# One decoder layer on one core: weight pieces of one megabyte, modulation vectors in one go, mixer constants in slots, decay columns apart

## The chip, the cores and the metric

The kernel runs on one core of a Trainium2 chip. The metric is the device time of one execution in microseconds: the median of several runs, three of the kernel before.

## What is computed

One layer of a decoder trunk for 256 tokens of width 2048, all in float32. A condition vector c is turned into six modulation vectors; the layer mixes tokens in three parallel branches (a causal pooling, a stick-breaking attention with 8 heads, a linear attention with 4 heads and a decay that depends on the data), gates and adds the branches, and ends with a gated feed-forward of width 5632.

```python
mod = silu_c @ w_ada + b_ada                    # shift, scale, gate, twice
h = _rmsnorm(x, g_norm1) * (1.0 + sc1) + sh1
proj = h @ w_in                                 # u_pool, q/k/v_sb, q/k/v/r_gla, a_low (16 columns), 3 x 2048 gates
log_alpha = log_sigmoid(a_low @ w_a2 + b_a2) / GLA_TAU
merged = sum_i sigmoid(g_i) * (branch_i @ W_br_i)
x = x + ga1 * (merged @ w_out)
h = _rmsnorm(x, g_norm2) * (1.0 + sc2) + sh2
x = x + ga2 * ((silu(h @ w_gate) * (h @ w_up)) @ w_down)
```

## The kernel before

**Products.** Everything is kept transposed: x and h are 16 chunks of 128 channels by 256 tokens. TensorE's float32r operands hold fewer bits than float32, so each operand is split into hi (a rounded copy, made by ScalarE) and lo (what is left, a subtraction on VectorE). `mm3` multiplies hi by hi, hi by lo and lo by hi in three matmuls of 256 columns; `mm2` does the first two in one matmul of 512 columns, since an operand's hi and lo lie side by side.

**Weight pieces.** `load` (L65) takes a buffer of `wraw`, which has six of 1056 columns (528 KB), and SP issues the DMA. `split_w` (L71) makes hi (L77) and lo (L78) of the whole piece, in `whi` and `wlo` with three buffers each; the raw buffer is free after lo. Nearly all pieces have 1024 columns, 512 KB: a block of 128 output columns over 2048 channels is two pieces. `w_per` has pieces of 768 columns, v of the linear attention pieces of 1056.

**Modulation vectors.** w_ada lies transposed, so each of the 96 columns of 128 channels is a product with c, which every partition holds, summed along the row: `ada_half` (L170) loads half a vector (512 KB) and VectorE multiplies and sums it in one instruction (L173); the second half starts from the sum of the first. The 32 vectors of the first norm are made in `modulate` (L211), the others from a queue, `ada_q`, some halves at each call of `ada` (L181): in `proj_v`, after each gate, after each branch block, after blocks of the output projection and after each `gated`.

**Stages, in the order of the program.**
- The first norm.
- For each chunk n: `modulate(n + 1)` in steps between the products of chunk n. `persistent` adds chunk n to six pairs of columns that stay in PSUM; from n = 4 on, `extra` makes 14 other pairs over groups of four chunks, summed in SBUF. At n = 14 the mixers' constants are loaded (L265).
- The last group of the 14 extra pairs (L539), each followed by `steps`, then v with the 16 columns of the decay's rank behind it (L544: 528 columns, as two halves of 264, in four accumulators), then the gates of the first eight blocks.
- The mixers are generators: a piece of work, then a `yield` with a cost. `steps(n)` (L497) runs up to n pieces of those that are due; each goes in two blocks or more after what feeds it. The linear attention's steps (`gla_level`, `gla_diagonal`, `gla_cross`) can't begin before `gla_decay` is through, and that waits for `gl["a"]`, which is set behind v (L553). It loads `w_a2` (L330) and turns the 16 columns round by matmuls with the identity (L333).
- The other gates, branch products and merge (L592); the output projection with the residual (L624 to L640, L632 is the last block's update of x); the second norm (L641), whose chunks `modulate2` makes; the feed-forward, whose first three blocks go chunk by chunk; and w_down (L682).

A scheduler puts the instructions of each engine in an order by its own estimate of when each is ready; instructions that come first in the program have priority. At run time each engine works through its queue in that order. `slots` has 62 buffers of 128x512 for everything else.

## Time and profile before

| | us |
|---|---|
| median of three runs | 1560.77 (1560.53 to 1561.52) |
| span of the profiled execution | 1558.6 |
| TensorE busy in it | 1518.9 (97%) |
| VectorE busy | 1130.8 (73%) |
| ScalarE busy | 739.7 (47%) |

The profile is of one execution, which has its own span, a little under the time of a run. DMA engines move 377 MB, 242 GB/s on average. A busy share is an average over stages with different limits, so the rows further down go by stretches: TensorE's gaps in each, what ended them, and what the other engines and the DMA queue did meanwhile. Times within the span are counted in microseconds from its start.

### The profile page before, as it was taken

Reading aid. Unit: us, or ns where it says so; the run is one execution under the profiler, and the core shown is the slowest. Engines: PE = TensorE matmul, PEld = TensorE weight load, DVE = VectorE, ACT = ScalarE, POOL = GpSimd, SP = SyncE. Lnnn points to the kernel's source line nnn. Section 1 sums busy time; section 2 is a strip of 40 time slices with the busy share of each in tenths; the row PEclk is TensorE's granted clock in tenths of the full one; section 3 lists DMA queues with packets and bytes.
Section 4 is the critical chain, followed back from the end, with each engine's and each line's share of the span. In section 5 each row is a group of like instructions: output and inputs, shape, how many; then the busy total and the mean of one; then the engine's idle time right before and its main releaser. Section 6 shows DMA issues by size and latency. Waiting matters only on the chain.

```text
span 1558.6 us, 26019 instructions
## 1 busy us (share of the span) xinstructions
PE 1518.9 (97%) x10304; PEld 1398.8 (90%) x10304; DVE 1130.8 (73%) x1671; ACT 739.7 (47%) x1028; POOL 1.9 (0%) x11
## 2 busy tenths in 40 slices
PE   5899999989999999999989999999999999999999
PEld 4899998989999999999877888888888888888888
DVE  7889979988877889898878666665555555545443
ACT  4454456465565434444445444444444444333333
POOL 0000000000000000000000000000000000000000
PEclk9899999999999999999999999999999999999999
DMA  9999984855768999997865777776666665666663
GB/s 329 372 328 326 332 276 136 287 193 194 243 215 280 323 342 345 351 314 230 285 208 196 234 239 229 241 230 188 189 189 189 188 189 176 207 192 202 190 207 95
DMA packets 108556, 377.17 MB, mean 242 GB/s; under 512 B 12049, under 2 KB 15249, under 8 KB 108433
## 3 DMA queue, kind: packets, MB, share of 16 engines
q1 hardware_dynamic: 108434, 375.52, 73.5%
q8 instruction: 80, 1.31, 0.3%
q14 instruction: 42, 0.34, 0.1%
HBM read 373.37 MB, written 2.10 MB: 241 GB/s over the span
## 4 chain that ended last, share of the span: by engine, by line
PE 91%; DVE 4%; DMA 2%; ACT 1%; issue 1%; SPq 0%; DVEq 0%; ACTq 0%
PE acc L108 34%; PE acc L109 18%; PE acc L92 9%; PE acc L90 9%; PE acc L91 9%; PE mx L90 3%; PE mx L91 3%; PE mx L92 3%; PE mx L239 3%; DVE raw L173 1%; PE acc L533 1%; DVE lo L78 1%; PE mx L377 1%; DMA raw<-in_w_ada_dram 1%; ACT s L39 1%
## 5 line engine op out<-in xcount | busy, mean ns | idle before, releaser
L78 DVE TENSOR_TENSOR lo<-raw,hi 128x1024 fp32r<-128x1024 f32 (+2 forms) x528 | 627.4, 1190 | 316.9 <-ACT hi L77 315.5
L77 ACT CAST hi<-raw 128x1024 fp32r<-128x1024 f32 (+2 forms) x528 | 539.3, 1023 | 653.6 <-issue 208.4
L108 PE MATMUL acc<-s,hi 128*128 128x512 f32 x2308 | 806.6, 394 | 5.5 <-DVE s L652 4.4
L109 PE MATMUL acc<-s,lo 128*128 128x256 f32 x2308 | 650.1, 282 | 1.2 <-DVE lo L78 1.1
L108 PEld LDWEIGHTS acc<-s,hi 128*128 128x128 f32 x2308 | 434.1, 188 | 104.5 <-issue 4.7
L109 PEld LDWEIGHTS acc<-s,lo 128*128 128x128 f32 x2308 | 434.7, 188 | 2.3 <-DVE lo L78 2.1
L90 PE MATMUL acc<-s,hi 128*128 128x256 f32 x1212 | 346.3, 286 | 14.2 <-ACT hi L77 14.1
L92 PE MATMUL acc<-s,lo 128*128 128x256 f32 x1212 | 344.6, 285 | 0.9 <-DVE lo L78 0.9
L91 PE MATMUL acc<-s,hi 128*128 128x256 f32 x1212 | 343.5, 284 | 0.0
L90 PEld LDWEIGHTS acc<-s,hi 128*128 128x128 f32 x1212 | 232.0, 191 | 16.3 <-ACT hi L77 15.6
L92 PEld LDWEIGHTS acc<-s,lo 128*128 128x128 f32 x1212 | 231.3, 191 | 2.9 <-DVE lo L78 2.2
L91 PEld LDWEIGHTS acc<-s,hi 128*128 128x128 f32 x1212 | 231.5, 191 | 0.2 <-issue 0.2
L173 DVE CUSTOM_DVE_ANT_0 raw<-raw,cs,mod 128x1024 f32<-128x1024 f32 x96 | 122.9, 1280 | 35.9 <-DMA raw<-in_w_ada_dram 35.1
L173 DVE CUSTOM_DVE_ANT_0 raw<-raw,cs,vt 128x1024 f32<-128x1024 f32 x96 | 122.8, 1279 | 29.3 <-DMA raw<-in_w_ada_dram 29.0
L90 PE MATMUL mx<-s,hi 128*128 128x256 f32 x384 | 110.0, 287 | 0.0
L91 PE MATMUL mx<-s,hi 128*128 128x256 f32 x384 | 108.3, 282 | 0.0
L92 PE MATMUL mx<-s,lo 128*128 128x256 f32 x384 | 108.0, 282 | 0.0
L39 ACT ACTIVATE s<-s 128x256 f32<-128x256 f32 (+2 forms) x167 | 83.5, 518 | 48.3 <-DVE s L662 34.7
L90 PEld LDWEIGHTS mx<-s,hi 128*128 128x128 f32 x384 | 73.2, 191 | 0.7 <-issue 0.5
L91 PEld LDWEIGHTS mx<-s,hi 128*128 128x128 f32 x384 | 72.8, 190 | 0.7 <-issue 0.7
L92 PEld LDWEIGHTS mx<-s,lo 128*128 128x128 f32 x384 | 72.7, 190 | 0.0
L239 PE MATMUL mx<-hi,s 128*128 128x256 f32 x256 | 47.4, 282 | 0.7 <-DVE s L302 0.7
(133 smaller groups left out, 780.5 us busy)
## 6 DMA issues: line engine op xcount, KB each, us to landing
raw<-in_w_ada_dram SPq DMA_DIRECT2D x192, 512.0 KB, 4.9
raw<-in_w_ff_dram SPq DMA_DIRECT2D x176, 512.0 KB, 4.2
raw<-in_w_gate_dram SPq DMA_DIRECT2D x96, 512.0 KB, 4.7
raw<-in_w_down_dram SPq DMA_DIRECT2D x80, 512.0 KB, 4.2
raw<-in_w_ext_dram SPq DMA_DIRECT2D x56, 512.0 KB, 5.2
raw<-in_w_br_dram SPq DMA_DIRECT2D x32, 512.0 KB, 5.0
raw<-in_w_out_dram SPq DMA_DIRECT2D x32, 512.0 KB, 4.5
raw<-in_w_per_dram SPq DMA_DIRECT2D x32, 384.0 KB, 5.0
```

The costliest lines, as they stand in the source:

```text
L39: r = nc.scalar.activation(out, in_, func, **kw)
L77: nc.scalar.copy(hi, raw)
L78: vec.tensor_tensor(lo, raw, hi.bitcast(F32), ALU.subtract)
L90: mm(out, lhsT=wh, rhs=x[:, :T], start=first, stop=False, skip_group_check=True)
L91: mm(out, lhsT=wh, rhs=x[:, T:], start=False, stop=False, skip_group_check=True)
L92: mm(out, lhsT=wl, rhs=x[:, :T], start=False, stop=last, skip_group_check=True)
L108: mm(out, lhsT=hi[:, k * P:(k + 1) * P], rhs=x, start=first, stop=False, skip_group_check=True)
L109: mm(out[:, :T], lhsT=lo[:, k * P:(k + 1) * P], rhs=x[:, :T], start=False, stop=last, skip_group_check=True)
L173: vec.tensor_tensor_reduce(raw, raw, cs[:, i * 1024:(i + 1) * 1024], 1.0, init, ALU.mult, ALU.add, mod[:, t, i:i + 1])
L239: mm(m[:, b * T:(b + 1) * T], lhsT=l, rhs=r, start=first and i == 0, stop=last and i == 2, skip_group_check=True)
L377: mm(m[:, i * w:(i + 1) * w], lhsT=k[:, i * P:(i + 1) * P], rhs=q[:, i * w:(i + 1) * w], start=True, stop=True)
L533: mm(m[b][c][:, :w], lhsT=xs, rhs=ws[:, o:o + w], start=f, stop=l)
```

## The change

`wraw` gets four buffers of 2048 columns (1 MB) instead of six of 1056. A weight piece is up to 1 MB, one block of 2048 channels; the class `Weights` loads it at once and splits it in parts of 1024 columns (768 in `w_per`), each when it is first used. A modulation vector is one load and one instruction over 2048 columns (for chunk 0 two of each); `ada` counts halves in `due` and takes a vector when two are due. `modulated` replaces the chunk's modulation in both norms: a product with scale and rstd on VectorE, the shift with rounding on ScalarE, the rest on VectorE. The constants (`ct`, `mneg`, `mk`, and `w_a2`) get slots and are loaded at n = 14. The decay's 16 columns leave v, which has 512 columns now in two accumulators; they get 16 matmuls of their own ahead of the last extra pieces, with 48 stationary columns (hi, zeros, lo) and the 512 columns of h, so they come out turned already. `extra` works on two pairs at a time.

```diff
-WW = 1056
+WW = 2048
+PART = 1024
-    wraw = ctx.enter_context(tc.tile_pool(name="wraw", bufs=6))
+    wraw = ctx.enter_context(tc.tile_pool(name="wraw", bufs=4))
...
-    def split_w(src):
...
+    class Weights:
+        def __init__(self, src, part=PART):
+            self.raw, self.part, self.made = load(src), part, {}
+
+        def at(self, col, n):
+            i = col // self.part
+            if i not in self.made:
+                raw = self.raw[:, i * self.part:min((i + 1) * self.part, self.raw.shape[-1])]
+                hi, lo = (p.tile([P, PART], F32R, tag=t, name=f"{t}{next(names)}")[:, :raw.shape[-1]]
+                          for p, t in ((whi, "hi"), (wlo, "lo")))
+                nc.scalar.copy(hi, raw)
+                vec.tensor_tensor(lo, raw, hi.bitcast(F32), ALU.subtract)
+                self.made[i] = hi, lo
+            col -= i * self.part
+            return tuple(p[:, col:col + n] for p in self.made[i])
...
-    def ada_half(t, i):
-        raw = load(w_ada[t, i])
-        init = vt[:, V_ADA + t:V_ADA + t + 1] if i == 0 else mod[:, t, 0:1]
-        vec.tensor_tensor_reduce(raw, raw, cs[:, i * 1024:(i + 1) * 1024], 1.0, init, ALU.mult, ALU.add,
-                                 mod[:, t, i:i + 1])
+    def ada_vec(t, parts=1):
+        raw = wraw.tile([P, WW], F32, tag="raw", name=f"raw{next(names)}")
+        w = D // parts
+        for i in range(parts):
+            nc.sync.dma_start(raw[:, i * w:(i + 1) * w], w_ada[t, :, i * w:(i + 1) * w])
+        for i in range(parts):
+            p = raw[:, i * w:(i + 1) * w]
+            vec.tensor_tensor_reduce(p, p, cs[:, i * w:(i + 1) * w], 1.0,
+                                     mod_col(t) if i else vt[:, V_ADA + t:V_ADA + t + 1], ALU.mult, ALU.add, mod_col(t))
...
     def ada(n):
+        due[0] += n
+        while due[0] >= 2 and ada_q:
+            due[0] -= 2
+            t = ada_q.popleft()
+            ada_vec(t)
...
+    def modulated(xk, g, r, b):
+        f, t = slot()[:, :T], slot(F32R)
+        vec.scalar_tensor_tensor(f, xk, g, r, ALU.mult, ALU.mult)
+        act(t[:, :T], f, AF.Identity, bias=b)
+        vec.scalar_tensor_tensor(t[:, T:], f, b, t[:, :T].bitcast(F32), ALU.add, ALU.subtract)
+        return t
...
         if n == 14:
-            nc.sync.dma_start(ct, consts)
+            ct, mneg, wa2 = slot()[:, :T], slot()[:, :384], slot()
+            mk = slot().bitcast(U8)[:, :1024].rearrange("p (a t) -> p a t", a=8)
+            tri, up = ct[:, :P], ct[:, P:]
+            nc.sync.dma_start(ct, consts[:, :T])
+            nc.sync.dma_start(mneg, consts[:, T:])
+            nc.sync.dma_start(wa2, w_a2)
...
-        wa2, aa = slot(), slot()
-        nc.sync.dma_start(wa2, w_a2)
-        m = mx()
-        for b in range(2):
-            mm(m[:, b * P:(b + 1) * P], lhsT=gl["a"][:, b * P:(b + 1) * P], rhs=ident, start=True, stop=True)
-        nc.scalar.copy(aa[:, :T], m[:, :T])
-        vec.memset(aa[32:33, :T], 1.0)
-        yield
+        aa = gl["a"]
...
-    for e in range(14):
-        extra(e, 3)
-        ready.add(e)
-        steps(ST2, 2.6)
-    m = proj_v(w_vg, 528)
-    at = slot()
...
-    gl["a"] = at
+    raw = load(w_a1)
+    hi = whi.tile([P, PART], F32R, tag="hi", name=f"hi{next(names)}")[:, :768]
+    nc.scalar.copy(hi, raw)
+    low = hi.rearrange("p (k c) -> p k c", c=48)[:, :, 32:]
+    vec.tensor_tensor(low, raw.rearrange("p (k c) -> p k c", c=48)[:, :, 32:], low.bitcast(F32),
+                      ALU.subtract)
+    m, aa, t = mx(), slot(), slot()
+    nc.gpsimd.memset(aa[:, :T], 0.0)
+    nc.gpsimd.memset(aa[64:65, :T], 1.0)
+    for k in range(NK):
+        mm(m[:48, :], lhsT=hi[:, k * 48:(k + 1) * 48], rhs=h[k], start=k == 0, stop=k == NK - 1)
+    nc.scalar.copy(t[:48, :T], m[:48, T:])
+    vec.tensor_tensor(aa[:48, :T], t[:48, :T], m[:48, :T], ALU.add)
+    gl["a"] = aa
+    for pair in range(7):
+        for e in extra(pair, 3):
+            ready.add(e)
+            steps(ST2, 2.6)
+    m = proj_v(w_vg, 512)
...
-    ada(len(ada_q) - 32 - 13 * ADA[3])
+    ada(2 * len(ada_q) - due[0] - 32 - 13 * ADA[3])
...
     for half in range(2):
-        w = [split_w(w_ff[j, i, half]) for j, i in firsts]
+        w = [Weights(w_ff[j, i, :, half * 1024:(half + 1) * 1024]) for j, i in firsts]
+        for p in w:
+            p.at(0, P)
```

## Rows read from the trace of the kernel before

**Rows 1.** The page's busy table: us, share of the span, instructions.
```profile
PE 1518.9 (97%) x10304; PEld 1398.8 (90%) x10304; DVE 1130.8 (73%) x1671; ACT 739.7 (47%) x1028; POOL 1.9 (0%) x11
```

**Rows 2.** Stretches: us, busy time by engine (PE first), PEclk, DMA share, GB/s.
```profile
28.00:56.00 28.00, 20.84 (x133) 19.10 (x132) 27.27 (x48) 9.87 (x16) 0.00 (x0) 0.86 0.99 374
56.00:60.00 4.00, 4.00 (x25) 4.00 (x25) 3.58 (x6) 2.12 (x3) 0.00 (x0) 0.67 1.03 412
80.00:235.00 155.00, 155.00 (x1308) 155.00 (x1307) 136.84 (x193) 75.07 (x96) 0.00 (x0) 1.00 0.91 316
235.00:283.00 48.00, 46.21 (x328) 41.31 (x326) 45.04 (x73) 32.50 (x51) 0.00 (x0) 1.00 0.52 164
283.00:317.00 34.00, 31.16 (x224) 28.37 (x223) 32.36 (x70) 16.71 (x26) 0.00 (x0) 1.00 0.75 250
317.00:480.00 163.00, 161.14 (x1328) 157.93 (x1328) 132.31 (x234) 97.20 (x159) 1.05 (x2) 1.00 0.69 221
480.00:700.00 220.00, 219.34 (x1837) 218.36 (x1836) 193.36 (x292) 95.56 (x122) 0.00 (x0) 1.00 0.93 330
804.00:834.00 30.00, 21.38 (x106) 16.81 (x104) 24.77 (x61) 15.92 (x25) 0.00 (x0) 0.89 0.37 125
```

**Rows 3.** Waits of TensorE over the span: us in total, times, longest.
```profile
PE acc L90 <- ACT hi L77: 14.1, 5, 7.2
PE acc L108 <- DVE s L652: 4.4, 1, 4.4
...
PE mx L340 <- DMA s<-in_w_a_dram: 1.7, 1, 1.7
PE mx L298 <- DVE s L481: 1.2, 1, 1.2
```

**Rows 4.** Timeline of VectorE around 42 us: start, us, instruction.
```profile
41.45 1.28 DVE L173 CUSTOM_DVE_ANT_0 raw<-raw,cs,mod 128x1024 f32<-128x1024 f32 x1
...
42.66 1.28 DVE L173 CUSTOM_DVE_ANT_0 raw<-raw,cs,vt 128x1024 f32<-128x1024 f32 x1
```

**Rows 5.** Groups by line, VectorE: busy us, mean ns, idle before.
```profile
L402 DVE TENSOR_TENSOR s<-s 128x512 f32<-128x512 f32 x14 | 9.6, 683 | 0.0
L387 DVE COPY_PREDICATED s<-mk,mx 128x64 f32<-128x64 uint8 x56 | 9.3, 247 | 4.4 <-PE mx L377 4.4
...
L134 DVE SCALAR_TENSOR_TENSOR s<-mx,s 128x512 f32<-128x512 f32 (+1 forms) x12 | 7.5, 641 | 5.1 <-ACT s L39 5.1
...
L406 DVE TENSOR_TENSOR s<-s,s 128x256 f32<-128x256 f32 x14 | 5.9, 421 | 1.6 <-ACT s L39 1.6
...
L294 DVE SCALAR_TENSOR_TENSOR s<-s,vt,s 128x256 f32<-128x256 f32 x8 | 3.8, 475 | 0.0
```

**Rows 6.** DMA issues by line: count, size, median us from issue to landing.
```profile
raw<-in_w_down_dram SPq DMA_DIRECT2D x80, 512.0 KB, 4.2
...
raw<-in_w_down_dram SPq DMA_DIRECT2D x16, 256.0 KB, 3.3
```

**Rows 7.** Pieces of the chain that ended last: start, us, what.
```profile
283.19 11.68 PE acc L533 x96
...
323.94 0.45 PE mx L333 x4
...
816.60 0.23 PE acc L108
```

**Rows 8.** Timeline around the second norm, TensorE and VectorE.
```profile
804.45 0.60 PE L642 MATMUL mx<-s,full 128*128 128x256 f32 x2
805.89 1.28 DVE L173 CUSTOM_DVE_ANT_0 raw<-raw,cs,mod 128x1024 f32<-128x1024 f32 x1 [1.87 <-DMA raw<-in_w_ada_dram]
...
807.10 0.48 DVE L632 SCALAR_TENSOR_TENSOR x<-acc,mod,x 128x256 f32<-128x256 f32 x1
...
822.87 1.28 DVE L173 CUSTOM_DVE_ANT_0 raw<-raw,cs,vt 128x1024 f32<-128x1024 f32 x1
...
825.34 0.40 PE L109 MATMUL acc<-s,lo 128*128 128x256 f32 x1 [0.39 <-DVE lo L78]
```

More of the change, by code (lines that the diff above doesn't have):

```diff
@@ L32 @@
 def kernel(ctx: ExitStack, tc: tile.TileContext, xT, c, vecs, consts, invc, masks, w_ada, w_per, w_ext,
-                      w_gate, w_vg, w_a2, w_pool, w_br, w_out, w_ff, w_down, outT):
+                      w_gate, w_vg, w_a1, w_a2, w_pool, w_br, w_out, w_ff, w_down, outT):
     nc = tc.nc
@@ L228, in extra @@
[L228 to L247 removed]
+        h.append(modulated(x[k], scl[:, k:k + 1], rstd, mod_col(k)))
@@ new lines, in persistent, with extra @@
+    def persistent(k):
+        w = Weights(w_per[k], 768)
+        for t in range(12):
+            mm3(per[t // 2][:, t % 2 * T:(t % 2 + 1) * T], w, t, h[k], k == 0 and t % 2 == 0, k == NK - 1)
+    def extra(pair, g):
+        w = Weights(w_ext[pair, g])
+        for e in (2 * pair, 2 * pair + 1):
+            m = mx()
+            for kk in range(4):
+                xk = h[4 * g + kk]
+                col = e % 2 * 1024 + kk * T
+                for b in range(2):
+                    first, last = kk == 0 and b == 0, kk == 3
+                    if 6 <= e < 10:
+                        xh, xl = xk[:, b * P:(b + 1) * P], xk[:, T + b * P:T + (b + 1) * P]
+                        wh, wl = w.at(col, T)
+                        for i, (l, r) in enumerate(((xh, wh), (xh, wl), (xl, wh))):
+                            mm(m[:, b * T:(b + 1) * T], lhsT=l, rhs=r, start=first and i == 0, stop=last and i == 2,
+                               skip_group_check=True)
+                    else:
+                        mm3(m[:, b * T:(b + 1) * T], w, col // P + b, xk, first, last)
+            if g == 0:
+                ext[e] = slot()
+                nc.scalar.copy(ext[e], m)
+            else:
+                vec.tensor_tensor(ext[e], ext[e], m, ALU.add)
+            yield e
@@ L255 @@
     for n in range(NK):
-        todo = [(persistent, n, 0), (persistent, n, 1)]
+        todo = [(persistent, n)]
         if n >= 4:
-            todo += [(extra, e, n // 4 - 1) for e in range(14 * (n % 4) // 4, 14 * (n % 4 + 1) // 4)]
+            todo += [(lambda p, g: run(extra(p, g)), p, n // 4 - 1) for p in range(7 * (n % 4) // 4, 7 * (n % 4 + 1) // 4)]
         nxt = modulate(n + 1) if n + 1 < NK else iter(())
@@ L594 @@
         sig = sigs[j]
-        hl = [split_w(w_br[j, i]) for i in range(2)]
+        w = Weights(w_br[j])
         brs = [acc(), acc()]
@@ L745, in _layouts @@
     ]
[L748 removed]
+_NAMES = ["xT", "c", "vecs", "consts", "invc", "masks", "w_ada", "w_per", "w_ext", "w_gate", "w_vg", "w_a1", "w_a2", "w_pool",
           "w_br", "w_out", "w_ff", "w_down"]
```

155 lines of the change are left out of this document (53 added, 102 removed).

## The prediction

> **What bounds the kernel now.** I read the busy table first, then the table of stretches, the waits of TensorE, and last the single instructions of the stretches where TensorE isn't full. TensorE is busy 97% of the span [rows 1], so at most 39.7 us of 1558.6 can be won without taking matmuls away. The table of stretches says where they lie [rows 2]: TensorE works 155.00 of 155 us between 80 and 235, and 219.34 of 220 between 480 and 700, and the feed-forward stage has next to no waits either. Weights that arrive in another grain can win nothing there. What is open: the start (20.84 of 28 us, and less before), the stage of the last extra pieces and of v (46.21 of 48 and 31.16 of 34), and the second norm (21.38 of 30). The list of waits agrees [rows 3]: 14.1 us for hi pieces (mostly the start), 4.4 at the second norm, 1.7 for `w_a2`, single waits of about a microsecond on VectorE's mixer steps. So the forecast is a sum of small terms in three places, plus the matmuls that are added.
>
> **The start.** The first chunks need, for each `n`, two modulation vectors (2 MB) and 768 KB of `w_per`. Which is late, the DMA or VectorE? Between 28 and 56 us both are full: VectorE 27.27 of 28 us, DMA share 0.99 at 374 GB/s [rows 2]. VectorE's queue there is a chain without holes: one reduction starts 1.21 us after the one before it [rows 4]. What of it is fixed? A 128x512 subtraction takes 683 ns and a 128x256 multiplication 421 ns [rows 5]: 262 ns for 256 columns, about 1.02 ns a column, and so 1.05 us of the 1.21 for 1024 columns and 0.16 us fixed. Summing a vector in one go saves that 0.16 once per vector, 0.3 us for each `n`. `modulated` gives back a little: two `scalar_tensor_tensor` at 475 ns for a multiplication and a subtraction of about 421 [rows 5], 0.1 us for each `n`. ScalarE loses a cast, but it waits for VectorE here. Net 0.2 us for four chunks (the first vectors stay in two parts), and some of VectorE's 0.7 us of gaps: **-1.0 us**. Bounds: -3.6 (rival 2, below) and +2, if a reduction has to wait for a whole megabyte. For that the rows give a price: 256 KB of `w_down` land in 3.3 us, 512 KB in 4.2 [rows 6], so I estimate 1 MB at 6.0. Four buffers of 1 MB hold more bytes than six of 528 KB, so the DMA queue is fed no worse, and I take the small gain.
>
> **Chunks 4 to 15, gates, feed-forward.** The splits stay 1024 columns wide (768 in `w_per`) and hi and lo keep three buffers, so TensorE's distance from VectorE is unchanged; casts and subtractions are the same in number, save half a column block in v. 0, with TensorE full as cover [rows 2]. If that cover fails it is rival 4. Fewer DMA issues on SP are worth nothing while TensorE is full.
>
> **Matmuls added and removed.** v takes 192 matmuls of 264 columns now; 96 of them last 11.68 us in the chain [rows 7], so all 23.4. After: 96 of 512 columns at 0.23 us, as such a one takes in the chain [rows 7]: 22.1. The decay's rank columns get 16 matmuls of 512 columns of their own, 3.7 us (if 48 stationary columns instead of 128 shortened it in proportion, 1.4; I keep 3.7, the row it is nearest to, since what streams are the 512 moving ones). Away go four transposing matmuls with the identity, 0.45 us [rows 7]. Net **+1.9 us**, all on TensorE.
>
> **The wait for `w_a2`.** Its load moves from `gla_decay` to chunk 14, several extra pieces before its use, so TensorE's 1.7 us at that place [rows 3] go: **-1.7 us**. What is late next there is the mixer step itself, in a stretch where TensorE has 161.14 of 163 us [rows 2]. The other loads at chunk 14 are in SP's queue before, too; `w_a2` adds 256 KB behind `w_per` of the next chunk, under a microsecond of DMA with buffers ahead.
>
> **The order of the mixers' steps.** This is the part with two answers. `gl["a"]` is set before the last extra pieces instead of behind v. Followed by hand through `steps`, the planner then puts the first halves of seven levels and of the crossing (L402, L406, and L407 like L402: 1.8 us of VectorE each [rows 5]), the decay's logarithms, the diagonal and four selections (four copies of L387 each [rows 5]) into the stretch from the first `extra(.., 3)` to the end of v. Together some 19.8 us. Out of it go the norms of heads 5 to 7 (about 2.6 us each: L134, two operations of its kind, two of L294 [rows 5]), and of four pool ends, four outputs and one step of head 5 another 6.3: 14.2. So +5.6 us of VectorE. Four vectors in one go, fewer copies of v and no memset take 1.3 back: +4.3 us, in a stretch where VectorE works 45.04 of 48 and 32.36 of 34 us already [rows 2]. Against that: 4.6 us are free in these 82; the a1 matmuls give VectorE 3.7 us of cover just ahead; and the waits behind v (1.2 us on L481 [rows 3], and one like it on L134) come from the pool and norm work that moves away; also v holds two accumulators instead of four, so a gate can start beside its copies. From +4.3 to -3.2 (all such waits gone). I take **0**, as the two lists balance.
>
> **The second norm.** The chain here [rows 8]: VectorE's reduction at 805.89 waited 1.87 us for a DMA, and the update of x[15] (L632) stood behind it and began at 807.10, though the matmuls behind that block's last one start at 804.45. So about 2.4 us of the path are a vector half that nobody needs yet (a gate of the feed-forward, asked for by the first `gated`) which got in front. After the change `due` counts: 94 halves are asked for by the end of the branches, 47 vectors; the next comes at j = 14, and the one after that only with the second `gated`, behind six half pieces and a whole one, with four buffers. It can't have landed by L632. The one at j = 14 is queued between w_out[14] and w_out[15], some ten microseconds ahead. **-2.4 us**; if a vector still gets in front, it costs 1.8 us more landing and 1.1 more reduction than now, +2.9. After that TensorE's first matmul waits 4.4 us [rows 3] for the norm's chain, whose length stays (multiply, activation, subtraction in both). VectorE has an operation less per chunk, which is worth nothing: TensorE waits for the first chunk alone (one wait in that row). At the half's end the reduction at 822.87 stands in front of lo and costs TensorE 0.4 us [rows 8]; gone: **-0.4**.
>
> **Sum.** -1.0 + 1.9 - 1.7 + 0 - 2.4 - 0.4 = -3.6 us on the span of 1558.6, so 1555.0. The median of the runs is 1560.8, 2.2 us over the span, which I keep: **1557.1 us**. A measurement of this kernel tells about 0.2% from no change, 3.1 us, so the forecast sits near that edge.
>
> **Rivals.**
> 1. *VectorE is the new bound of the mixers' stage.* For it: the 95% above, and the slots. Counting live slots in program order, `ct`, `mneg`, `wa2`, `mk` and the steps that start early raise the peak from 55 to 62, of 62 there are; at the peak an operation, or a pool's load on SP with weights queued behind it, waits for another's end. It decides once VectorE's 4.6 free us can't take 4.3 more. Price 4.3 us, up to 8 with slots: 1561 to 1565, slower. Against: in the gates' stretch VectorE has 132.31 of 163 us. In this rival's stretch the Trainium skill would look for the same sign: its page Perfetto Trace Analysis (section Identifying Performance Opportunities) says that a gap that repeats on the engine that should be full can mean that no buffer is free for the next tile. No run here shows it for slots yet.
> 2. *The pieces are faster, and the start with them.* In 56 to 60 us the DMA moved 412 GB/s [rows 2]; with that instead of 374 over 28 us the start is 2.6 us shorter: 1554.5. Against it: VectorE's 27.27 of 28. The Trainium skill (DMA: Bandwidth & Descriptors, section Bandwidth) has a rule for this: batch to at least 1 MiB for 75% of the peak, which by its table would put 512 KB clearly lower. The trace doesn't agree: many 512 KB pieces in flight hold a share of 0.99, so the grain isn't what holds them back.
> 3. *The late vector doesn't go, another takes its place* (what the change does to the queue is decided by the scheduler's order, not by the text): the -2.4 becomes 0 to +2.9, 1559.5 to 1562.4.
> 4. *Coarse pieces starve TensorE* where VectorE and DMA are both near full (80 to 235, 480 to 700: share 0.91 and 0.93 [rows 2]): a reduction that waits 1.8 us longer, with lo pieces behind it. Lo is two pieces ahead, which covers one such wait and not several: +5 to +8, 1562 to 1565.
>
> **How the numbers follow.** Forecast 0.45 (its own range 1554 to 1560: 0.27 faster, 0.18 the same); rival 1 0.22 (0.07 the same, 0.15 slower); rival 2 0.13 (faster); rival 3 0.12 (0.09 the same, 0.03 slower); rival 4 0.08 (slower). Faster 0.40, the same 0.34, slower 0.26. The range goes from 1552, where rival 2 meets the mixers' good end, to 1565.
>
> **What would show it.** Start: VectorE's reductions about 2.3 us apart and TensorE full a microsecond earlier. v: 96 matmuls of 512 columns, then 16 with 48 stationary ones. No wait on `w_a2`. L632's place: no reduction in front of it. In the mixers' stage: VectorE above 95% and TensorE's waits on lo or mixer steps above 5 us would be rival 1. Waits on hi or lo between 80 and 235 or 480 and 700 would be rival 4. I'm wrong in the step and not the size if the second norm's wait stays, or if TensorE isn't full in a stretch that is full now.

## The result, and the profile after

The changed kernel takes 1573.57 us (median of four runs, 1571.07 to 1586.23), the kernel before in the same comparison 1561.14 us: a ratio of 1.0102, interval 1.0079 to 1.0125. It is slower by 12.4 us; forecast was 1557.1 with a range up to 1565. The profiled execution has a span of 1571.0 us, 12.4 more than before. One thing has to be known to read the numbers below: executions of one and the same kernel of this family can lie in two groups 12 to 14 us apart (three of these four runs are in the lower one, 1586.23 is in the upper), which in the profiles differ in the feed-forward, so that a median or a ratio can be of either group or of a mixture. So I locate gains and losses by stages, each from one profiled execution.

The busy table after the change:

```profile
PE 1525.0 (97%) x10220; PEld 1400.9 (89%) x10220; DVE 1117.2 (71%) x1464; ACT 728.6 (46%) x1010; POOL 2.5 (0%) x13
```

TensorE has 84 matmuls fewer than before [rows 1], and is busy 6 us longer. The table of stretches after (us, busy time by engine from TensorE on, granted clock, DMA share, GB/s), in windows of [rows 2]:

```profile
28.00:56.00 28.00, 18.62 (x132) 17.36 (x131) 25.44 (x34) 8.01 (x12) 0.00 (x0) 0.93 0.97 353
...
80.00:235.00 155.00, 154.29 (x1286) 154.12 (x1285) 132.15 (x156) 68.95 (x84) 0.53 (x1) 1.00 0.86 313
...
283.00:317.00 34.00, 32.83 (x203) 28.69 (x202) 32.08 (x63) 20.82 (x33) 0.00 (x0) 1.00 0.58 202
```

Read two things. Between 28 and 56 us VectorE, which had 27.27 us of work in 28, now has 25.44: it idles, and TensorE with it (for what, is shown further down). And between 80 and 235 us TensorE is busy for 154.29 of 155 us, 0.7 less than before, but has done 22 matmuls fewer, which at 0.12 us each is 2.6 us: the same busy time holds fewer matmuls. TensorE's waits over the span (us in total, times, longest), to be laid beside [rows 3]:

```profile
PE acc L101 <- DVE lo L85: 12.1, 8, 3.0
PE acc L99 <- ACT hi L84: 9.3, 3, 6.7
...
PE acc L553 <- DVE lo L85: 3.3, 2, 2.7
...
PE acc L99 <- ACT s L40: 1.6, 1, 1.6
PE acc L100 <- DVE s L209: 1.2, 1, 1.2
PE acc L553 <- ACT hi L84: 1.1, 1, 1.1
PE mx L670 <- ACT s L40: 0.9, 1, 0.9
```

The wait on `w_a2` is gone. The hi waits of the start fell from 14.1 to 9.3, but 12.1 us on lo (L85) stand there new; v (L553) waits 4.4 us, which before it didn't; L670 is the second norm's last matmul (L643 before) and waits 0.9, where L643 waited 3.0.

**Three landmarks** serve for every comparison below. A: the first VectorE copy of a persistent accumulator (L274 before, L300 after), which ends the first stage. B: the start of the second norm's last matmul. C: the last update of `x`. All in us.

| kernel | A | A to B | B to C | C |
|---|---|---|---|---|
| before | 213.1 | 595.0 | 747.3 | 1555.4 |
| after | 223.7 | 601.1 | 743.1 | 1567.9 |
| difference | +10.6 | +6.1 | -4.2 | +12.5 |

So the loss is in the first stage and in the mixers' and branches' stages. The feed-forward gave some back in this execution, which is of the lower group; kernels whose profile is of the upper group have 755 to 758 for B to C.

### The profile page after: what moved, and what is told of

Read it like the earlier page. It is cut to its first block, busy times and chain, and to the rows that moved or that the text cites. A ratio compares the mean times of both kernels' runs of the same rounds, so it can differ in the third digit from the quotient of the medians.

```text
span 1571.0 us, 24822 instructions
## 1 busy us (share of the span) xinstructions
PE 1525.0 (97%) x10220; PEld 1400.9 (89%) x10220; DVE 1117.2 (71%) x1464; ACT 728.6 (46%) x1010; POOL 2.5 (0%) x13
## 4 chain that ended last, share of the span: by engine, by line
PE 90%; DVE 6%; DMA 2%; ACT 1%; issue 1%; DVEq 0%; ACTq 0%
PE acc L118 34%; PE acc L119 17%; PE acc L101 9%; PE acc L100 8%; PE acc L99 8%; PE mx L99 2%; PE mx L100 2%; PE mx L101 2%; PE mx L259 2%; DVE raw L187 2%; DVE lo L85 1%; DMA raw<-in_w_ada_dram 1%; PE mx L396 1%; ACT s L40 1%; PE acc L553 1%
## 5 line engine op out<-in xcount | busy, mean ns | idle before, releaser
L85 DVE TENSOR_TENSOR lo<-raw,hi 128x1024 fp32r<-128x1024 f32 (+1 forms) x528 | 627.9, 1192 | 376.3 <-ACT hi L84 375.5
L84 ACT CAST hi<-raw 128x1024 fp32r<-128x1024 f32 (+1 forms) x528 | 539.6, 1024 | 664.5 <-PE acc L118 225.6
L99 PE MATMUL acc<-s,hi 128*128 128x256 f32 x1212 | 347.0, 287 | 10.8 <-ACT hi L84 9.3
L101 PE MATMUL acc<-s,lo 128*128 128x256 f32 x1212 | 345.6, 287 | 12.1 <-DVE lo L85 12.1
L99 PEld LDWEIGHTS acc<-s,hi 128*128 128x128 f32 x1212 | 235.0, 194 | 12.8 <-ACT hi L84 10.4
L187 DVE CUSTOM_DVE_ANT_0 raw<-raw,cs,vt 128x2048 f32<-128x2048 f32 (+1 forms) x96 | 223.1, 2325 | 14.4 <-DMA raw<-in_w_ada_dram 14.4
L40 ACT ACTIVATE s<-s 128x512 f32<-128x512 f32 (+2 forms) x165 | 82.6, 521 | 71.4 <-DVE s L684 53.4
L99 PE MATMUL mx<-s,hi 128*128 128x256 f32 x384 | 109.7, 286 | 0.8 <-DVE s L267 0.7
L99 PEld LDWEIGHTS mx<-s,hi 128*128 128x128 f32 x384 | 73.7, 192 | 1.8 <-issue 1.1
L259 PEld LDWEIGHTS mx<-hi,s 128*128 128x128 f32 x256 | 40.3, 192 | 0.2 <-DVE s L144 0.2
```

The costliest lines, as they stand in the source:

```text
L40: r = nc.scalar.activation(out, in_, func, **kw)
L84: nc.scalar.copy(hi, raw)
L85: vec.tensor_tensor(lo, raw, hi.bitcast(F32), ALU.subtract)
L99: mm(out, lhsT=wh, rhs=x[:, :T], start=first, stop=False, skip_group_check=True)
L101: mm(out, lhsT=wl, rhs=x[:, :T], start=False, stop=last, skip_group_check=True)
L187: vec.tensor_tensor_reduce(p, p, cs[:, i * w:(i + 1) * w], 1.0, mod_col(t) if i else vt[:, V_ADA + t:V_ADA + t + 1], ALU.mult, ALU.add, mo ...
```

## The experiments

Theories. S: the start is late because of the grain, the buffers or the order of the work. P: TensorE's spacing is changed by where its operands lie in SBUF, which the change moves (hi and lo shrink from 1056 to 1024 columns, constants leave their tiles, the raw buffers change). M: the early decay makes VectorE the bound at v (rival 1). Rival 4: coarse pieces starve TensorE behind the start.

**Grain undone (e1_grain).**

```
-    wraw ... bufs=4   # tiles of 2048 columns
+    wraw ... bufs=8   # tiles of 1024 columns
-            self.raw, self.part, self.made = load(src), part, {}
+            self.raw = [load(src[:, i:min(i + part, n)]) for i in range(0, n, part)]
-    def ada_vec(t, parts=1):
+    def ada_vec(t, parts=2):   # each half in a buffer of its own
```

> The changed kernel with its raw buffers in the old grain: eight buffers of 1024 columns instead of four of 2048 (the same bytes), every piece loaded in parts of 1024 columns, every modulation vector in two loads and two reductions. Everything else of the change stays (decay apart, constants in slots, modulated, extras in pairs, 62 slots). Theory A, the grain of the pieces makes the loss: the copies of the six pairs in PSUM, which begin at 223.7 us in the changed kernel and at 213.1 before, come back to 212 to 215, the last branch block's first product (732.6 after, 714.9 before) to 717 to 721, and the run to 1558 to 1564 us. Theory B, the order of the extras makes it (chunk 4 has one pair, so TensorE runs dry before chunk 5 is modulated): the copies stay at 220 or later and the run at 1569 or more. Theory C, the decay's earlier place and the slots make it: the copies come back, but the loss between them and the branch stage (some 3 us) stays and grows nothing here; 1562 to 1566.

1583.63 us, ratio 1.0146 (1.0112 to 1.0180). A 218.3, A to B 609.8, B to C 754.9. The old grain gives 5.4 us back at the start (2.4 against the earliest profile of the changed start, 220.7 in e4_late) and then costs 8.7 us behind it. Rival 4 said the reverse of the second.

**Vectors in halves alone (e2_halves).**

```
-    def ada_vec(t, parts=1):
+    def ada_vec(t, parts=2):
```

> The changed kernel with each modulation vector in two loads of 512 KB and two reductions of 1024 columns, in one buffer of 1 MB as before this edit; weights stay in pieces of 1 MB. It takes away the long reduction and the wait for a whole vector, but not the coarse buffers. Theory A1 (VectorE's long reductions block the subtractions and chunk results behind them): most of the 10 us at the start come back, copies at 213 to 217, 1560 to 1565 us. Theory A2 (the buffers' number is what counts, four instead of six, and so the order in which SP can issue): copies stay at 220 to 225, 1569 to 1576 us.

1582.62 us, ratio 1.0135 (1.0094 to 1.0176); three of its four runs are in the upper group. A 220.7, A to B 602.3. As a cause by itself it can't be told from nothing: e4_late, whose first stage is the changed kernel's to the letter, has A at 220.7 too, so a single profile tells nothing under 3 us there.

**Extras 4, 4, 4, 2 (e3_pairs).**

```
-  for p in range(7 * (n % 4) // 4, 7 * (n % 4 + 1) // 4)]
+  for p in range(-(-7 * (n % 4) // 4), -(-7 * (n % 4 + 1) // 4))]
```

> The changed kernel with the seven pairs of extra pieces spread as 2, 2, 2, 1 over each group of four chunks instead of 1, 2, 2, 2; nothing else. Theory B (chunk 4 has too little work while chunk 5 is being modulated): the gap of TensorE between 68.9 and 72.7 us goes, and with it its second slow clock stretch, 4 to 7 us in all; 1566 to 1569. Theory A (the grain): the second pair's megabyte comes in front of chunk 5's vector on the DMA queue, so that chunk comes later by about 2.7 us and what TensorE wins in work it loses in waits: 1570 to 1576.

1578.28 us, ratio 1.0123 (1.0082 to 1.0164). By 80 us it has done 340 matmuls where the changed kernel has 295, but by 210 us it has 1371, as many as that. (Its copies come at 229.3 since one pair more, 48 matmuls, stands ahead of them.) More extras in the first group only move the gap to later chunks.

**The decay handed on behind v (e4_late).**

```
-    gl["a"] = aa          # ahead of the last extras
     m = proj_v(w_vg, 512)
     ...
+    gl["a"] = aa
```

> The changed kernel with the decay's columns handed to the mixers behind v, as before, instead of ahead of the last extra pieces; the 16 matmuls stay where they are. The linear attention's steps then run after v again and fewer slots are live at once. Forecast's rival 1 (VectorE bound in the mixers' stage by the early steps, slots at 62): the stretch from the copies to the first branch product, 298.8 us in the changed kernel and 296.2 before, shrinks by 2 us or more: 1568 to 1571. Theory that the order is worth nothing, as the forecast took it: within 1.5 us of the changed kernel.

1579.88 us, ratio 1.0133 (1.0116 to 1.0151); it sits in the upper group (B to C 756.4). A 220.7, A to B 595.5 against 601.1: 5.6 us, and two more kernels with the early decay and narrow tiles have 602.3 (e2_halves) and 600.3 (e9_between). So handing the decay on early costs that, and v's waits on lo and hi are gone from its list; whether VectorE's work makes the price, as M says, or the slots, this run doesn't separate.

**Hi and lo wide again (e5_wide).**

```
-  hi, lo = (p.tile([P, PART], F32R, tag=t, ...
+  hi, lo = (p.tile([P, 1056], F32R, tag=t, ...
```

> The changed kernel with the tiles of hi and lo 1056 columns wide as before the change (1024 of them used), nothing else: hi at byte 76992 with a pitch of 4224 instead of 4096 bytes, lo and the slots moved by 384 and 768 bytes. Theory A (where the operands lie in SBUF sets TensorE's spacing): 256-column matmuls again 118.7 ns apart on average instead of 120.0 in full stretches, 172 instead of 169 of them in 80 to 100 us, and the total 6 to 7 us shorter, about 1565. Theory B (the spacing comes from something else in the change): 120.0 ns and 169 as in the changed kernel, total 1571 to 1586.

1573.55 us (1573.22 to 1574.43), ratio 1.0079 (1.0059 to 1.0099). The spacing of 256-column matmuls loses its fixed 120 ns (171 of them in 80 to 100 us, 169 in the changed kernel), A to B falls from 601.1 to 596.9, but B to C is 749.9: what the early stages win the feed-forward loses, so the total doesn't move. The place matters; the expected total of 1565 was wrong.

**The kernel before with narrow tiles (e6_narrow).**

```
-WW = 1056
+WW = 1024
-            hi, lo = split_w(src[i])
             for kk in range(2):
+                hi, lo = split_w(src[i][:, kk * n:(kk + 1) * n])
```

> The kernel before with the tiles of raw, hi and lo 1024 columns wide; so that v's pieces fit they come as 16 of 528 columns instead of 8 of 1056. Nothing else is changed. Theory A (place in SBUF sets the spacing): 256-column matmuls 120.0 ns apart, 169 in 80 to 100 us, total about 1565, perhaps with two levels 12 us apart. Theory B: 118.7 ns and 172, total 1558 to 1560 (eight more splits in v cost at most a microsecond).

1565.46 us (1563.13 to 1580.52), ratio 1.0046 (1.0017 to 1.0075). P holds without anything else of the change but narrower raw tiles and v's smaller pieces, though A, at 213.8, moves by 0.7 us only. Two matmuls of the timeline, a hundred apart, in the kernel before (start, us, instruction):

```profile
99.74 0.29 PE L92 MATMUL mx<-s,lo 128*128 128x256 f32 x1
...
111.62 0.28 PE L90 MATMUL mx<-s,hi 128*128 128x256 f32 x1
```

and in e6_narrow:

```profile
99.75 0.28 PE L90 MATMUL mx<-s,hi 128*128 128x256 f32 x1
...
111.75 0.28 PE L91 MATMUL mx<-s,hi 128*128 128x256 f32 x1
```

11.88 against 12.00 us. B to C is 743.9, as in the changed kernel, and the same kernel also ran 1575.27, 1578.74 and 1580.52: the two groups come with the place, too.

**The old start as a whole (e7_start).** On top of e1_grain each half of a vector, each half of the persistent piece and each single extra is back in its place:

```
-        todo = [(persistent, n)]
+        todo = [(persistent, n, 0), (persistent, n, 1)]
-            todo += [... p in pairs, 2, 4, 4, 4 extras to a chunk]
+            todo += [... e one by one, 3, 4, 3, 4 to a chunk]
```

> e1_grain (the changed kernel with loads and reductions of 512 KB in 8 buffers) with the order of the kernel before in the first stage too: each half of a vector, each half of the persistent piece and each single extra piece in its old place in the program, extras 3, 4, 3, 4 to a chunk. Theory C (the start is lost by the order: two reductions in a row ahead of the lo pieces, and a first group of extras that is smaller): the copies of the persistent accumulators, at 213.1 before, 223.7 changed, 218.3 in e1_grain, come at 215 (1.7 of it for the spacing of 120 ns), and the total falls by 3 against e1_grain. Theory D (the shift and the two-operand form of modulated make VectorE's cycle longer): they stay at 218.

1583.80 us, ratio 1.0142 (1.0112 to 1.0172). A 213.4: the start is whole again, even at 120 ns. A to B is 608.4, as in e1_grain. C against D: the order. Two things have to be kept apart here. All these kernels start 1485 matmuls ahead of A; in e7_start TensorE is idle for 20.3 us up to there (before 19.6, e1_grain 22.4) and busy for 193.1 (193.5, 195.9). The idle time is the order's. That the busy time is no longer than before in spite of the 120 ns goes with the clock: granted in 20 to 80 us are 0.97 here and 0.91 in the other two (means of stretches at 1.2 and 2.4 GHz), and one trace doesn't tell whether the order or the execution made that. `modulated`, which is in e7_start, adds no idle time on VectorE in the first four chunks in this order.

**Three good parts in the kernel before (e8_parts).**

```
+    def modulated(xk, g, r, b): ...      # as in the change, in both norms
+            wa2 = slot(); nc.sync.dma_start(wa2, w_a2)     # at chunk 14
-        ada(1)                           # in gated
+        if len(hid) > 2:
+            ada(1)
```

> The kernel before with three parts of the change alone: modulated in both norms, the load of w_a2 at chunk 14, and the reductions of the feed-forward's vectors two gated blocks later (none in front of the update of x[15]). Tiles, pieces and order stay. By the forecast's terms: w_a2 -1.7, second norm -2.4, modulated 0, so 1558.2 - 4.1 = 1554. If modulated lengthens VectorE's cycle in the first chunks (0.58 us a chunk for the wait on ScalarE's shift, five chunks): 1557.

1557.92 us (1554.79 to 1558.80), ratio 0.9980 (0.9967 to 0.9993): faster than both kernels. A 212.4 (-0.7: TensorE's idle time ahead of A grows by 1.2 us, its busy time falls by 1.9 at a granted clock of 0.97 in 20 to 80 us, before 0.91), A to B 593.3 (-1.7), B to C 747.6. Inside A to B the stretch from the last branch product to B fell from 93.2 to 91.1 us, near the 2.4 of the forecast. The wait on `w_a2` is gone as well, and more than given back in the mixers' stage: its list of waits has

```profile
PE acc L92 <- DVE lo L78: 3.1, 7, 1.1
...
PE mx L305 <- DVE s L487: 1.5, 1, 1.5
...
PE mx L485 <- PE mx L299: 1.0, 1, 1.0
```

where before the change lo at L92 cost 0.9 in all, and the waits that answer to L487 and L485 were 1.2 [rows 3] and 0.5. (Of the 3.1 us on lo 1.5 lie in the mixers' stage, the rest in the first.)

**The second vector between the halves, at 1 MB (e9_between).**

```
-    def persistent(k):            # all twelve blocks
+    def persistent(k, i):         # six, and a vector ahead of each call
-        todo = [(persistent, n)]
+        todo = [(persistent, n, 0), (persistent, n, 1)]
```

> The changed kernel, pieces of 1 MB and all, but in the first stage the persistent piece's two halves go in one after the other with a vector in front of each (vector, half, vector, half) as before the change, instead of vector, both halves, vector. Theory C (the order: the second vector's reduction stands behind both lo halves, which wait for ScalarE, which waits for TensorE): the copies of the persistent accumulators come at 215 to 217 instead of 220.7 to 223.7, the total at 1565 to 1568. Theory G (the grain: a reduction that waits for a whole megabyte): they stay at 221 or later.

1582.68 us, ratio 1.0143 (1.0125 to 1.0161), upper group. A 220.1, against 220.7 to 223.7 for the changed start: the order of whole vectors is worth 0.6 to 3.6 us, which a single profile can't tell from nothing.

**Place: e10_pitch, e11_shift, e12_shift128.** All three are e8_parts with the tiles of hi and lo 1152 columns wide; the last two have 256 and 128 unused bytes between lo and the slots.

```
-        hi = whi.tile([P, WW], F32R, ...      # lo likewise
+        hi = whi.tile([P, 1152], F32R, ...
+    nc.gpsimd.memset(pad_p.tile([P, 64], F32, ...), 0.0)     # e11_shift; 32 in e12_shift128
```

> e8_parts with hi and lo tiles 1152 columns wide (4608 bytes, nine times 512) instead of 1056, nothing else: hi, lo and the slots then all start at the same place modulo 512 bytes, as they do in the changed kernel and in e6_narrow, but no longer a power of two apart. If what fixes the spacing is that all operands are a multiple of 512 bytes apart: 120.0 ns without spread, total 1561 to 1564. If it is the pitch of 4096: spread around 118.7 as before, 1557 to 1558.

> e10_pitch with 256 unused bytes in front of the slots, so that weights and moving operands lie half of 512 bytes apart, the same for every buffer. If the relative place of weights and moving operand sets the spacing, it is another fixed value than in e10_pitch, above or below 120.0 ns (117 would be 1551, 122 would be 1568); if only the pitch matters, the same as e10_pitch.

> e10_pitch with 128 unused bytes in front of the slots. As e11_shift: by the theory of the relative place a fixed value of its own, by the theory of the pitch the same as e10_pitch and e11_shift.

e10_pitch: 1572.11 us (1557.53 to 1573.80), ratio 1.0038 (1.0007 to 1.0069); four of its runs are at 1557.5 to 1559.4 and six at 1571.5 to 1573.8. e11_shift: 1571.95 (1571.63 to 1573.74), ratio 1.0074 (1.0057 to 1.0091). e12_shift128: 1563.32 (1561.97 to 1566.80), ratio 1.0023 (1.0013 to 1.0034). Against e8_parts nothing but unused columns and bytes has changed, and the median moves by 5 us and more. With hi, lo and slots equal modulo 512 bytes (e10_pitch) 256-column matmuls are 120.0 ns apart without spread; half of 512 off (e11_shift) they take 117, 118, 120 and 124 ns in equal parts and average 120.0 again; a quarter off, 118.7 early and 119.8 in the gates. So it isn't the pitch of 4096, and the relative place doesn't give each case a value of its own, as the theory had it.

**Halves interleaved at 1 MB (e13_interleaved).** On top of e9_between:

```
-            ada_vec(t, 2 if k == 0 else 1)
-            yield
+            for i in range(2):      # half a buffer each
+                nc.sync.dma_start(p, w_ada[t, :, i * 1024:(i + 1) * 1024])
+                vec.tensor_tensor_reduce(p, p, ...)
+                yield
```

> e9_between with the vectors in halves too (two loads into the halves of a 1 MB buffer, two reductions of 1024 columns), each half's reduction in its old place between the pieces; the weight pieces stay at 768 KB and 1 MB. If the vectors' grain and its order made the start late: the copies of the persistent accumulators at 214 to 216. If it is the weights' grain and four buffers: 219 or later, with waits of TensorE on lo of 2 to 3 us as in the changed kernel.

1595.40 us, ratio 1.0226 (1.0202 to 1.0249). A 236.7, 13 us later than the changed kernel. "219 or later" covers that, but not the reason given for it: TensorE waits 0.3 us on lo there, and 20.1 on hi (L99). What differs from e7_start is that the extras come as pairs and that weights come in 768 KB and 1 MB through four buffers; the next run tries the pairs alone.

**Pairs in the old start (e14_pairs).**

```
-            todo += [... e one by one, 3, 4, 3, 4 to a chunk]
+            todo += [(lambda p, g: run(extra(p, g)), p, n // 4 - 1) for p in ...]
```

> e7_start (512 KB everywhere, old order) with the extras as in the changed kernel, pair by pair, 2, 4, 4, 4 to a chunk instead of 3, 4, 3, 4. If the smaller first group lets TensorE run dry: the copies at 217 or later (213.4 in e7_start). If the vectors' order is what matters: 213 to 215.

1590.28 us, ratio 1.0192 (1.0148 to 1.0235). A 225.5: 12.1 us for the extras alone. TensorE's idle time ahead of A grows by 7.1 of them (27.4 us against 20.3); the other 5.0 are busy time for the same 1485 matmuls, in a trace in which the granted clock falls again after the gaps (0.93 in 80 to 130 us, where e7_start has 1.00). Three windows show where. e7_start:

```profile
0.00:60.00 60.00, 39.74 (x207) 30.97 (x208) 50.96 (x87) 23.14 (x35) 1.49 (x11) 0.97 0.96 358
60.00:80.00 20.00, 20.00 (x169) 20.00 (x168) 16.94 (x25) 9.93 (x14) 0.00 (x0) 1.00 1.00 382
80.00:210.00 130.00, 130.00 (x1086) 130.00 (x1085) 119.50 (x172) 56.35 (x68) 0.00 (x0) 1.00 0.95 335
```

e14_pairs:

```profile
0.00:60.00 60.00, 39.45 (x205) 30.68 (x206) 50.80 (x86) 22.19 (x34) 1.49 (x11) 0.97 0.95 357
60.00:80.00 20.00, 18.18 (x150) 17.78 (x149) 16.29 (x23) 9.21 (x13) 0.00 (x0) 1.00 0.97 355
80.00:210.00 130.00, 124.97 (x1006) 123.77 (x1005) 113.23 (x165) 54.42 (x67) 0.00 (x0) 0.97 0.91 315
```

The changed kernel:

```profile
0.00:60.00 60.00, 35.19 (x174) 28.06 (x175) 48.14 (x66) 21.21 (x33) 1.49 (x11) 0.93 0.93 344
60.00:80.00 20.00, 17.27 (x123) 16.86 (x122) 13.23 (x14) 7.25 (x9) 0.00 (x0) 0.86 0.83 304
80.00:210.00 130.00, 129.29 (x1078) 129.12 (x1077) 114.95 (x135) 58.01 (x72) 0.00 (x0) 1.00 0.89 324
```

and the kernel before:

```profile
0.00:60.00 60.00, 40.42 (x195) 33.05 (x196) 50.22 (x87) 25.17 (x40) 0.86 (x9) 0.91 0.94 348
60.00:80.00 20.00, 20.00 (x171) 20.00 (x170) 16.18 (x22) 11.36 (x16) 0.00 (x0) 1.00 0.95 342
80.00:210.00 130.00, 130.00 (x1098) 130.00 (x1097) 119.30 (x174) 61.55 (x79) 0.00 (x0) 1.00 0.95 335
```

The changed kernel falls behind it by 21, 48 and 20 matmuls in the three windows. In the first 60 us halves and their old order are worth 31 to 33 matmuls, with singles or pairs. From 60 us on, when extras begin, the pairs take 99 matmuls away in e14_pairs. The mechanism is in e14_pairs' timeline of VectorE (start, us, instruction, idle before and its releaser):

```profile
85.69 1.28 DVE L237 CUSTOM_DVE_ANT_0 raw<-raw,cs,mod 128x1024 f32<-128x1024 f32 x1
...
90.36 1.23 DVE L87 TENSOR_TENSOR lo<-raw,hi 128x1024 fp32r<-128x1024 f32 x1 [3.38 <-ACT hi L86]
92.31 1.23 DVE L87 TENSOR_TENSOR lo<-raw,hi 128x1024 fp32r<-128x1024 f32 x1 [0.73 <-ACT hi L86]
93.46 1.28 DVE L237 CUSTOM_DVE_ANT_0 raw<-raw,cs,vt 128x1024 f32<-128x1024 f32 x1
```

L237 is the reduction of half a vector. The next half, at 93.46, stands in program order behind a pair's two lo pieces, and those wait for hi. The next chunk's `h` can't come before it, so TensorE uses up the pair and waits.

**The three suspects undone (e15_undone).** e7_start with hi and lo 1056 wide and `gl["a"]` behind v (the edits of e5_wide and e4_late).

> e7_start with hi and lo 1056 columns wide and the decay's columns handed on behind v: the three suspects undone, everything else of the change kept (a1's matmuls, v in 512 columns, second norm, sums by due, constants in slots). If these three are the whole loss: spread around 118.7 ns, the first branch product at 508 to 511 us, the second norm 2 us shorter, total 1556 to 1560. If something else in the change costs: above 1563.

1572.06 us, ratio 1.0072 (1.0057 to 1.0087). A 212.0, as before the change; but A to B 603.7 and B to C 751.2. The three aren't the whole loss of this kernel. Of its waits (5.0 of the 6.1 us in the first row lie behind the first stage; L675 is the second norm):

```profile
PE acc L103 <- DVE lo L87: 6.1, 8, 1.4
...
PE mx L675 <- ACT s L40: 3.2, 1, 3.2
```

**Old start, large pieces behind it (e16_hybrid, e17_late_wide).** e17_late_wide is the changed kernel with the edits of e4_late and e5_wide. e16_hybrid adds the old start, its halves two to a 1 MB buffer:

```
+    def half(i, src):
+        if i == 0:
+            held_per[0] = wraw.tile([P, WW], F32, tag="raw", ...)
+        r = held_per[0][:, i * 1024:i * 1024 + n]
+        nc.sync.dma_start(r, src)
```

> The changed kernel with the first stage as before the change (vectors, persistent pieces and single extras in halves of 512 KB, two halves to a 1 MB buffer, extras 3, 4, 3, 4), hi and lo 1056 columns wide and the decay handed on behind v; from the last extras on the 1 MB pieces of the change. If the start, the place in SBUF and the early decay are the three costs, and 1 MB pieces do no harm behind the start: copies of the persistent accumulators at 212 to 214, from there to the second norm's matmul 591 to 595 us (603.7 in e15_undone), total 1554 to 1560. If the 1 MB pieces harm there: over 600 us for that stretch, total above 1563.

> The changed kernel with hi and lo 1056 columns wide and the decay handed on behind v (e4_late and e5_wide together), its start untouched. Copies of the persistent accumulators at 220 to 223 as in these two, then 591 to 595 us to the second norm's matmul, total 1564 to 1569: some 10 us above e16_hybrid, which is the start alone.

e16_hybrid: 1564.92 us (1564.52 to 1566.50), ratio 1.0034 (1.0020 to 1.0048); A 217.1, A to B 593.3, B to C 751.0. e17_late_wide: 1571.22 (1569.27 to 1572.05), ratio 1.0076 (1.0061 to 1.0091); A 222.9, A to B 593.6, B to C 750.6. Both totals miss their expectation, and so does A in e16_hybrid (212 to 214), though A to B is as expected. Behind the start 1 MB pieces do no harm: 593.6 against 603.7 for 512 KB pieces. And the start is 5.8 us better with the old order of halves and single extras (idle ahead of A: 22.8 us against 28.2), 5.1 more (e15_undone, idle 19.4) with eight buffers that come free one by one. In the first 60 us of e16_hybrid

```profile
0.00:60.00 60.00, 38.83 (x188) 30.27 (x189) 48.66 (x83) 21.41 (x33) 1.49 (x11) 0.94 0.89 327
```

the DMA engines are busy 0.89 of the time at 327 GB/s, where e7_start has 0.96 and 358. With four buffers that are released as a whole, loads are asked for later: the DMA queue's longest wait for a buffer in 20 to 80 us is 5.0 us, in e7_start 2.9.

## Why the prediction was wrong, step by step

**The start: the step that failed.** Forecast -1.0 (bounds -3.6 to +2), measured +10.6. I costed VectorE's queue as a sum of operations, and its first term was right: a reduction of 2048 columns is followed by the next instruction after 2.27 us (69.92 to 72.19), 0.15 less than two starts 1.21 apart [rows 4]. What it left out is the order in that queue and the place of the extras, for which I wrote no term: the diff turns 3, 4, 3, 4 single extras into 2, 4, 4, 4 in pairs, and halves with other operations between them into whole vectors. VectorE's waits in 20 to 80 us after the change:

```profile
DVE lo L85 <- ACT hi L84: 6.4, 3, 3.4
DVE s L209 <- ACT s L40: 2.9, 5, 0.6
DVE raw L187 <- DMA raw<-in_w_ada_dram: 0.3, 1, 0.3
```

Two of these rows name the step. The second is the shift of `modulated`: "ScalarE loses a cast, but it waits for VectorE here" was half of it, for VectorE then waits for ScalarE, 0.58 us in each of the first five chunks, since nothing stands between the vector's reduction and the rest of `modulated`; four of the five make 2.3 of the 2.6 us that VectorE idles between 28 and 56 us. With vectors in halves the row all but goes (0.3 us in e1_grain). The first row was 3.5 us before the change. The changed kernel's VectorE at 65 us:

```profile
67.78 1.83 DVE L85 TENSOR_TENSOR lo<-raw,hi 128x768 fp32r<-128x768 f32 x2 [2.50 <-ACT hi L84]
69.52 0.48 DVE L207 SCALAR_TENSOR_TENSOR s<-x,scl,s 128x256 f32<-128x256 f32 x1
69.92 2.35 DVE L187 CUSTOM_DVE_ANT_0 raw<-raw,cs,vt 128x2048 f32<-128x2048 f32 x1
```

and its ScalarE:

```profile
66.42 0.59 ACT L265 COPY s<-mx 128x512 f32<-128x512 f32 x1 [5.30 <-PE mx L101]
66.91 1.57 ACT L84 CAST hi<-raw 128x768 fp32r<-128x768 f32 x2
```

The vector that TensorE needs next (69.92) stands behind two lo pieces, these behind their hi, that behind a copy which waits 5.30 us for TensorE's matmuls of the extra. A ring of in-order queues: TensorE feeds the copy, and waits in the end for what is queued behind it (1.57 and 1.16 us, at 70.60 and 72.72). So the unit of the price isn't the 0.16 us of an operation but the time of an extra, 24 matmuls of 0.12 us.

Up to A, before and after:

```profile
0.00:213.09 213.09, 193.51 (x1485) 186.13 (x1486) 187.51 (x284) 99.83 (x136) 0.86 (x9) 0.98 0.95 340
0.00:223.66 223.66, 195.41 (x1485) 187.71 (x1486) 185.60 (x224) 91.80 (x120) 2.02 (x12) 0.97 0.88 325
```

The matmuls are the same in number. Of the 10.6 us 8.7 are idle time (28.3 against 19.6) and 1.9 busy time; the spacing, 0.12 us more for each hundred, would make 1.8 us of that if all 1485 ran at the full clock, an estimate from above. The experiments give 5.8 us to the order with its extras (e17_late_wide to e16_hybrid) and 2.4 to 5.4 to the grain with its buffers (e1_grain against the four profiles of the changed start, A 220.7 to 223.7). The two don't add up cleanly: the old order of halves with pairs is worse than either (e13_interleaved, e14_pairs), because a half then stands behind a whole pair. Bound +2, "a reduction has to wait for a whole megabyte", was the wrong mechanism: VectorE's wait for the DMA is the 0.3 us of the third row. Rival 2, faster pieces, fell: 344 GB/s in the first 60 us after the change, 348 before. The Trainium skill (DMA: Bandwidth & Descriptors, section Bandwidth) asks for batches of at least 1 MiB; no run here shows a faster start by it, as e7_start with 512 KB pieces moves 358 GB/s in that window. The same bytes of buffers, in pieces that come free one by one, moved more; that the earlier requests are the reason is argued from the buffers, not shown by a run of its own.

**Chunks 4 to 15, gates, feed-forward: 0 forecast.** Wrong on two counts. The spacing: A to B lost 4.2 us by the place (e5_wide against the changed kernel; 1.9 between e4_late and e17_late_wide), and the feed-forward won 3.4 (e6_narrow). That gain is luck of the group: three of e6_narrow's ten runs and one of the changed kernel's four are in the upper one. That TensorE was full was no cover, since a full TensorE can run slower. And rival 4 is refuted: behind the start 1 MB pieces are better by 8.7 to 10.1 us in this kernel (e1_grain against the changed one, e15_undone against e17_late_wide). The kernel before, with 512 KB pieces too, takes 595.0 there; one thing that these two have and it hasn't is that `due` asks for a vector's two halves at once, which wasn't undone by itself. One place in e15_undone's VectorE:

```profile
544.03 1.28 DVE L186 CUSTOM_DVE_ANT_0 raw<-raw,cs,vt 128x1024 f32<-128x1024 f32 x1 [0.82 <-DMA raw<-in_w_ada_dram]
...
545.24 1.22 DVE L87 TENSOR_TENSOR lo<-raw,hi 128x1024 fp32r<-128x1024 f32 x1
```

The half's reduction waits for its load in front of a lo piece, and TensorE waits 1.06 us for that. At the second norm it is the same (813.47, 2.00 us for the load, in front of the update of `x`).

**Matmuls, +1.9.** The 16 of a1 are there with 48 stationary columns:

```profile
L570 PE MATMUL mx<-s,hi 128*48 128x512 f32 x16 | 3.8, 393 | 0.0
```

16 starts 0.23 apart, 3.7 us as taken; stationary columns don't shorten it.

**The wait on `w_a2`, -1.7.** It went (no such row after), but alone it isn't worth 1.7: in e8_parts lo and mixer steps took up the time, and A to B won no more than the second norm did. "What is late next" was named and priced at nothing.

**Mixers' order, 0 from -3.2 to +4.3.** Wrong value, at the upper end of the bounds or beyond: 5.6 us (e4_late) or 3.3 (e5_wide to e17_late_wide), about the 4.3 of rival 1. Its place was v: the 3.3 and 1.1 us on lo and hi at L553, absent when the decay comes late. VectorE is at 32.08 of 34 us there, 94%, not above 95 as I had asked. I had balanced the price against waits that would go (L481, L134); 1.2 and 1.1 us went and didn't outweigh it. Whether the slots have a share wasn't tried.

**The second norm, -2.4 and -0.4: right.** Before the change TensorE's wait there was

```profile
PE mx L643 <- ACT s L39: 3.0, 1, 3.0
```

and after it 0.9 (L670 above): 2.1 us. The wait on lo at the half's end is gone as well. VectorE at that place after the change:

```profile
821.62 1.23 DVE L85 TENSOR_TENSOR lo<-raw,hi 128x1024 fp32r<-128x1024 f32 x1 [1.31 <-ACT hi L84]
823.50 0.48 DVE L659 SCALAR_TENSOR_TENSOR x<-acc,mod,x 128x256 f32<-128x256 f32 x1 [0.65 <-PE acc L101]
```

No reduction stands in front of L659 (L632 in [rows 8]), which waits for TensorE alone. But the reason that I gave was half of it: counting by `due` isn't enough, since with 512 KB pieces (e15_undone) a half still gets in front and TensorE waits 3.2 us. Rival 3 fell.

**What is left.** With start, decay and place taken out, A to B is 593.6 (e17_late_wide) against 595.0 before: -1.4, where the terms of the sum for that stretch gave +1.9 - 1.7 - 2.4 = -2.2. So the terms of that stretch hold in sum, within what one profile tells, if not one by one; the loss is in the start and in what I had put at nothing: the order of the mixers' steps and the pace of a full TensorE.

## What to carry to other kernels

Where a stage has no slack, follow one period of it through all the in-order queues and ask for each operand what stands ahead of it and what that waits for; the sum of an engine's operations doesn't tell this. Splitting or merging pieces changes that order even where each piece's cost stays. And when a change moves or resizes tiles in SBUF, compare matmuls per 20 us in a full stretch first: a busy share of 1.00 hid 1 to 2% here (118.8 against 120.0 ns, and the two levels below).

## What the hardware showed that I had not expected

TensorE's pace depends on where hi, lo and the moving operands lie. Mean spacing of 256-column matmuls in full stretches: 118.8 ns before, with a spread of 112 to 127, and 120.0 in the changed kernel, e6_narrow and e10_pitch. In the feed-forward (512 and 256 columns in turn) a hundred matmuls of the kernel before take

```profile
949.79 0.28 PE L109 MATMUL acc<-s,lo 128*128 128x256 f32 x1
...
967.22 0.28 PE L109 MATMUL acc<-s,lo 128*128 128x256 f32 x1
```

17.43 us, of the changed kernel

```profile
949.70 0.39 PE L118 MATMUL acc<-s,hi 128*128 128x512 f32 x1
...
967.03 0.39 PE L118 MATMUL acc<-s,hi 128*128 128x512 f32 x1
```

17.33, and of e10_pitch in its profiled execution

```profile
949.82 0.28 PE L109 MATMUL acc<-s,lo 128*128 128x256 f32 x1
...
967.49 0.28 PE L109 MATMUL acc<-s,lo 128*128 128x256 f32 x1
```

17.67, at the full clock in all three. 17.33 and 17.67 are two levels that one kernel can run at: over the feed-forward they are the 12 to 14 us between the two groups of executions (B to C 743 to 744, or 755 to 758). e14_pairs, at 752.4, goes from one to the other within its profiled execution: a matmul of 512 and one of 256 columns take together 352.5 ns on average between 900 and 1090 us, 346.7 from 1330 on; e7_start goes the other way, from 347.0 to 353.3. The kernel before and e8_parts ran between the two, at 348.6, and e5_wide at 350.3. Whether an execution takes the one or the other, and why the place matters, none of these runs tells; that stays open.
